# A grouped-query attention kernel: a third block of every job's exponentials on VectorE, converted inside its own job, with one step of the correction moved from GpSimd to VectorE in each second job

## The chip, the cores and the metric

The kernel runs on one core of one Trainium2 chip. The metric is the device time of one execution in microseconds (us); the number quoted for a kernel is the median of several runs. One execution is also recorded by the hardware profiler; its timeline is what the views below are taken from.

## What is computed

```python
batch, seq, n_heads, n_kv_heads, dim = 8, 512, 32, 8, 64
scale = 1.0 / np.sqrt(dim)
K_expanded = np.repeat(K, n_heads // n_kv_heads, axis=2)
V_expanded = np.repeat(V, n_heads // n_kv_heads, axis=2)
# each of Q, K_expanded, V_expanded then as (batch, heads, seq, dim)
scores = np.einsum('bhqd,bhkd->bhqk', Q, K_expanded) * scale
weights = np.exp(scores - np.max(scores, axis=-1, keepdims=True))
weights = weights / (np.sum(weights, axis=-1, keepdims=True) + 1e-10)
output = np.einsum('bhqk,bhkd->bhqd', weights, V_expanded)
return output.transpose(0, 2, 1, 3).astype(np.float32)
```

Softmax attention over 512 positions, 8 batches, 32 query heads; four query heads share one head of keys and values. Inputs and output are fp32.

## The kernel before, in words

**Jobs.** The work is cut into 64 jobs, j = 0 to 63, eight for each batch. A job is four query heads, as two pairs (`i` = 0, 1) of two heads (`m` = 0, 1). For each pair there are four key chunks of 128 (`kc`). One combination of i, kc and m is a block: scores of 128 keys by 512 queries, one PSUM bank. A job has 16 blocks. Scores stand with the keys on the partitions, so the exponentials can be used as the stationary operand of the second product without a transpose. No maximum is subtracted; sums that leave safe bounds would lead to a general path at the end, which does not run here.

**Two ways to an exponential.** Most blocks go through ScalarE (ACT): `act_tile` (L296) lets PE compute two blocks into an s tile (two PSUM banks, two buffers) and ACT write exp of 1024 columns to the fp16 tile `pt`. The first two or three blocks of a job's second pair go another way, through VectorE (DVE) and GpSimd (POOL). `exp_d` (L306) lets PE compute them into a d tile (two banks, one buffer), and VectorE converts the scores to an integer, `u`, whose bits are those of a fp16 number that is a rough exponential. `exp_d2` (L320) works out a correction: `f` takes the low ten bits of u (VectorE), `g` is a linear function of f (GpSimd, or VectorE where `odd` is true), `w` is the product of g and f (GpSimd). In the job that follows, `exp_d4` (L346) adds u and w into `pt` (VectorE). `WIDE` (L41) says in which jobs there are three blocks: those from 4 to 61 but for j % 5 = 2, 47 in all. `act_tiles` (L252) gives ACT the rest: seven tiles of two blocks in a job with two blocks on VectorE; with three, six such tiles and a half tile of one block.

**Second product.** `pv` (L365) multiplies `pt` of the job before (`last`) by the values, 32 products per pair. V has a column of ones, so the sums of the weights come out beside the output. All pairs share one pv tile (two banks, one buffer). `norm` (L402) reads it: a reciprocal of the sums (L417) and a multiplication into `o_sb` (L422), from where each second job a DMA on the SP queue stores 1 MB.

**Order.** The instructions of each engine run in the order in which the program writes them; there is no scheduler. The loop at L570 writes job j in this order: loads on the POOL queue that are due in this job (`LOADS`), transposes of keys on the SP queue (`dma_k`, `KEYS`), ACT tile 0, the d tile's first two blocks and their u, ACT tile 1, checks (`check_sums` looks at earlier sums, `check_v` at a part of V, both on VectorE), products of the last job's first pair around ACT tile 2, its norm, ACT tile 3. Then a second d tile, called `bank`: with three blocks, ACT's half tile goes to its second bank (`act_tile(j, 4, bank)`), and eight PE transposes of the Q of job j + 2 (`trans_q`, L207) go to its first. VectorE then has: add of the last job (L349), f (L325), the copy of the transposed Q out of the bank (L220), and g if it is VectorE's in this job (`rest`). PE goes on with products of the last job's second pair in parts (`cut`) around the tiles 5 and 6. If the next job has three blocks, the third of them is computed in this job already, into the second bank after ACT has read it, and VectorE converts it (L622). The norm of the second pair ends the job.

**Reuse.** Tiles wait for their readers: a new d tile for VectorE's and ACT's reads of the one before, a pv tile for the norm before. `apart` (L200) declares that two instructions are in different banks of one tile and need not wait for each other.

**Where g stands before.** `odd` is true in job 62 and in jobs with three blocks whose successor has two (6, 11, ... 56, 61).

Of the kernel before, what the change touches and what calls it, by code (L numbers as in the profile page):

```python
# [12 lines left out]
FP32 = mybir.dt.float32  # L13
BF16 = mybir.dt.bfloat16
# [23 lines left out]
LAST_SUMS = NLAST * 2 * 4  # L38


WIDE = lambda j: 4 <= j < 62 and j % 5 != 2  # L41


@with_exitstack
# [23 lines left out]
def fast_path(ctx, tc, Q, K, V, out, flag, ident):  # L68
# [78 lines left out]
    def d_tile():  # L147
        return d_pool.tile([128, 2, S], FP32, name="d_ps")
# [51 lines left out]
    def apart(this, other):  # L200
        if other is not None:
            tc.declare_no_dep(
                this.ins, other.ins, reason="the two are in different banks of one tile"
            )
        return this
# [40 lines left out]
    def taken(j):  # L246
        return 3 if WIDE(j) else 2

    def d_block(j):
        return SC * 2 - 2 if j == NJOB - 1 else 0  # L250

    def act_tiles(j):  # L252
# [7 lines left out]

    CHECKS = {
        (j, at): divmod(n, SC) for n, (j, at) in enumerate(
            [(j, 0) for j in (3, 4, 6, 7, 8, 11, 12, 16, 17, 21, 22, 23, 26, 27, 31, 32)]
            + [(j, 0) for j in (36, 37, 38, 41, 42, 46, 47, 48, 51, 52, 56, 57, 60, 61, 62)]
            + [(62, 1)]
        )
    }

    KEYS = dict(zip((4, 10, 16, 26, 36, 41, 50), range(1, B)))

    def in_jobs(load, first, jobs):
        for n, j in enumerate(jobs):
            LOADS.setdefault(j, []).append((load, first + n))

    LOADS = {1: [(load_q, 1, 0, 2 * HPG), (load_q, 1, 2 * HPG, 4 * HPG)]}
    in_jobs(load_k, 1, [3, 8, 12, 23, 32, 38, 48])
    in_jobs(load_q, 2, [3, 7, 8, 12, 17, 22, 23, 27, 32, 37, 38, 42, 47, 48])
    in_jobs(load_v, 1, [4, 13, 18, 28, 33, 43, 53])

    def scores(j, ps, i, kc, m):  # L280
        u, g = divmod(j, 2)
        b, gp = divmod(u, GP)
        keys = kt_first[:, gp, :, :] if u < 2 else kt[b][:, :, gp, :]
        return nc.tensor.matmul(  # L284
            ps,
            keys[64 * m:64 * m + 64, g if u == 0 else g ^ m, kc * 128:(kc + 1) * 128],
            qt[u][64 * m:64 * m + 64, g, i, :],
            start=True,
            stop=True,
        )  # L290
# [2 lines left out]
        pt = pt_pool.tile([128, NPAIR, SC, 2, S], FP16, name="pt")  # L293
        jobs.setdefault(j, {}).update(pt=pt, pv={})

    def act_tile(j, n, spare=None):  # L296
        group = act_tiles(j)[n]
        i, kc, lo = group[0]
        ps = s_pool.tile([128, 2, S], FP32, name="s_ps") if spare is None else spare
        for _, _, m in group:  # L300
            scores(j, ps[:, m, :], i, kc, m)
        return nc.scalar.activation(  # L302
            out=jobs[j]["pt"][:, i, kc, lo:, :], in_=ps[:, lo:, :], func=EXP, scale=scale
        )

    def exp_d(j, lo, hi, ps, other=None):  # L306
        st = jobs.setdefault(j, {})
        if "u" not in st:
            for name, dtype in (("u", I16), ("f", I16), ("g", BF16), ("w", BF16)):
                st[name] = dve_pool.tile([128, 3, S], dtype, name=name + "16")[:, 0:taken(j), :]  # L310
        for n in range(lo, hi):
            apart(scores(j, ps[:, n - lo, :], DPAIR, *divmod(d_block(j) + n, 2)), other)
        return lambda: nc.vector.tensor_scalar(  # L313
            out=st["u"][:, lo:hi, :], in0=ps[:, 0:hi - lo, :], scalar1=A_U, scalar2=B_U,
            op0=ALU.mult, op1=ALU.add,
        )

    def exp_d2(j, engine=None):  # L320
        st = jobs[j]
        by_bits = engine is None
        engine = engine or nc.gpsimd
        odd = j == NJOB - 2 or WIDE(j) and not WIDE(j + 1)
        nc.vector.tensor_single_scalar(  # L325
            out=st["f"], in_=st["u"], scalar=1023, op=ALU.bitwise_and
        )

        def factor():
            (nc.vector if odd else engine).tensor_scalar(  # L330
                out=st["g"], in0=st["f"], scalar1=-EXP_F1,
                scalar2=EXP_K * 2.0 ** (24 * by_bits), op0=ALU.add, op1=ALU.mult,
            )

        def product():
            engine.tensor_tensor(  # L336
                out=st["w"], in0=st["g"], in1=st["f"].bitcast(FP16) if by_bits else st["f"],
                op=ALU.mult,
            )

        if odd:
            return lambda: (factor(), product())
        factor()
        return product() if by_bits else product
# [210 lines left out]
    for filler in fillers:  # L555
        apart(copy, filler)
    two_keys(1)
    exp_d(0, 0, 2, d_tile())()
    act_tile(0, 3)
    act_tile(0, 4)  # L560
    exp_d2(0)
# [8 lines left out]
    for j in range(1, NJOB - 1):  # L570
        last = j - 1
        u, g = divmod(j, 2)
        b, gp = divmod(u, GP)
        open_job(j)
        if j == 1:
            nc.gpsimd.tensor_copy(out=gate, in_=jobs[0]["pt"][0:1, 0, SC - 1, 0, 0:1])
        for load, *of in LOADS.get(j, ()):
            load(*of)
        if j == 1:
            dma_k(0, 2)  # L580
        if j in KEYS:
            dma_k(KEYS[j])

        cut = (11, 19) if taken(j) < 3 else (4, 18) if taken(last) < 3 else (4, 16)
        act_tile(j, 0)
        if j == 1:
            piece(1, *first_k(1, 0, bank[:, 1, S // 2:]))
        exp_d(j, 0, 2, d_tile())()
        act_tile(j, 1)
        if j % 5 == 3:  # L590
            check_sums()
        if (j, 0) in CHECKS:
            check_v(*CHECKS[j, 0])
        pv(last, 0, 0, 16)
        act_tile(j, 2)
        pv(last, 0, 16, 32)
        norm(last, 0)
        act_tile(j, 3)

        reads = []  # L600
        bank = d_tile()
        beside = act_tile(j, 4, bank) if taken(j) > 2 else None

        ahead = (j + 1,) if j < 2 else (3, 4) if j == 2 else (j + 2,)
        for n, to in enumerate(ahead):
            if to < NJOB:
                reads.append(trans_q(to, bank[:, n, :], other=beside)[1])
        if j == 1:
            reads.append(first_k(1, 1, bank[:, 1, :])[1])
        exp_d4(last)  # L610
        rest = exp_d2(j)
        copies = [read() for read in reads]
        if rest:
            rest()
        if taken(j) == 2:
            act_tile(j, 4)
        pv(last, 1, 0, cut[0])
        act_tile(j, 5)
        if beside:
            pv(last, 1, *cut)  # L620
        if taken(j + 1) > 2:
            exp_d(j + 1, 2, taken(j + 1), bank[:, 1:2, :], copies[0])()  # L622
        if (j, 1) in CHECKS:
            check_v(*CHECKS[j, 1])
        if not beside:
            pv(last, 1, *cut)
        act_tile(j, 6)
        pv(last, 1, cut[1], 32)
        norm(last, 1)
        del jobs[last]  # L630
# [1 line left out]
    j, last = NJOB - 1, NJOB - 2  # L632
    open_job(j)
    act_tile(j, 0)
    exp_d(j, 0, 2, d_tile())()
    all_checks()
    act_tile(j, 1)
    pv(last, 0, 0, 16)
# [137 lines left out]
```

## Time and profile before

| | |
|---|---|
| median of 3 runs | 404.32 us (403.99 to 404.6) |
| the profiled execution, its time | 404.57 us |
| its span, first to last instruction | 402.8 us |
| PE: matmul busy, granted clock | 375.8 us (93%), 0.999 |
| PE weight loads busy | 228.0 us (57%) |
| ACT wide tiles (128x1024), count and mean | 400, 1122 ns |
| ACT half tiles (128x512), count and mean | 47, 724 ns |
| DMA over the span | 168 GB/s |

The profile gives for each engine the time in which at least one of its instructions ran. A record lasts until the engine's last write is acknowledged, and the next instruction starts before that, so records of one engine overlap: 400 ACT tiles of 1122 ns come to 379.0 us busy. For the pace of an engine the distance from start to start is read off the timeline. In a row of the timeline the columns are the start, the duration, the engine, the line, the operation, what is written and read, and the count; in brackets stands idle time of the engine ahead of it and what ended that. The chain of waits is followed back from the last instruction, at each step to what released it.

### The profile page before, as it was taken

What the parts mean: (1) busy time and instruction counts of PE and PEld (TensorE: products, weight loads), DVE (VectorE), ACT (ScalarE), POOL (GpSimd) and SP (SyncE); (2) the same over time, 40 slices, a digit from 0 to 9 for tenths busy, and PEclk for the clock granted to TensorE, in tenths of its full rate; (3) what the DMA queues carried; (4) which work ended last, traced back from release to release, by engine and by line L of the source; (5) the groups of instructions that cost most, each with busy time, mean ns of one, the idle gap of its engine ahead of it and who ended that gap; (6) DMA issues with size and microseconds to landing.
All of it is one profiled execution on the core that took longest, in us unless ns stands there. A gap on an engine that the chain in (4) does not pass through costs nothing.

```text
span 402.8 us, 12997 instructions
## 1 busy us (share of the span) xinstructions
PE 375.8 (93%) x5670; PEld 228.0 (57%) x5670; DVE 366.4 (91%) x635; ACT 393.9 (98%) x454; POOL 286.8 (71%) x169
## 2 busy tenths in 40 slices
PE   7999999999999999999999999999999999999985
PEld 3565555555555555555555555555555555556554
DVE  4788998999999999999999999999999999999996
ACT  5999999999999999999999999999999999999995
POOL 9848577597587687687687686677776767765752
PEclk9999999999999999999999999999999999999999
DMA  9979999899999259999259999679369959222206
GB/s 145 163 190 182 91 288 225 164 211 237 184 214 206 107 88 247 192 239 182 107 84 226 168 227 197 208 109 252 110 170 202 175 169 128 107 106 106 88 34 201
DMA packets 82893, 67.73 MB, mean 168 GB/s; under 512 B 52752, under 2 KB 57872, under 8 KB 82832
## 3 DMA queue, kind: packets, MB, share of 16 engines
q0 software_dynamic: 45072, 24.91, 48.3%
q1 hardware_dynamic: 36688, 41.49, 36.6%
q8 instruction: 45, 0.74, 0.7%
q10 hardware_dynamic: 1072, 0.46, 0.4%
q14 instruction: 16, 0.13, 0.1%
HBM read 50.33 MB, written 33.55 MB: 208 GB/s over the span
## 4 chain that ended last, share of the span: by engine, by line
ACT 29%; PE 25%; POOL 24%; DVE 20%; issue 2%; ACTq 0%; DVEq 0%
ACT pt L302 28%; POOL w L336 16%; PE pv L377 12%; PE s_ps L284 9%; POOL g L330 8%; DVE pt L349 8%; DVE o_sb L422 4%; DVE f L325 4%; DVE qt L220 2%; PE d_ps L215 2%; DVE g L330 1%; DVE inv L417 1%; PE d_ps L284 1%; PE s_ps L510 1%; PE d_ps L377 0%
## 5 line engine op out<-in xcount | busy, mean ns | idle before, releaser
L302 ACT ACTIVATE pt<-s_ps 128x1024 f16<-128x1024 f32 x400 | 379.0, 1122 | 0.3 <-PE s_ps L284 0.2
L336 POOL TENSOR_TENSOR w<-g,f 128x1536 bf16<-128x1536 bf16 (+1 forms) x63 | 179.6, 2851 | 37.6 <-DVE g L330 33.4
L377 PEld LDWEIGHTS <-pt 128*128 128x128 f16 x4096 | 142.1, 98 | 81.2 <-issue 41.6
L377 PE MATMUL pv<-v,pt 128*128 128x65 bf16 x4032 | 177.8, 195 | 3.7 <-DVE o_sb L422 2.2
L284 PE MATMUL s_ps<-qt,kt 64*128 64x512 bf16 x746 | 152.3, 384 | 12.0 <-ACT pt L302 10.0
L330 POOL TENSOR_SCALAR g<-f 128x1536 bf16<-128x1536 int16 (+1 forms) x50 | 67.1, 1341 | 69.1 <-DVE f L325 69.0
L313 DVE TENSOR_SCALAR u<-d_ps 128x1024 int16<-128x1024 f32 (+1 forms) x111 | 109.9, 990 | 0.3
L284 PEld LDWEIGHTS <-kt 64*128 64x128 bf16 x960 | 50.2, 93 | 55.3 <-issue 31.5
L422 DVE TENSOR_TENSOR o_sb<-pv,inv 128x512 f32<-128x512 f32 x112 | 77.5, 692 | 3.9
L284 PE MATMUL d_ps<-qt,kt 64*128 64x512 bf16 x214 | 58.4, 376 | 3.5 <-ACT pt L302 0.3
L349 DVE TENSOR_TENSOR pt<-u,w 128x1536 uint16<-128x1536 int16 (+1 forms) x64 | 56.4, 882 | 2.3 <-POOL w L336 0.2
L220 DVE COPY qt<-d_ps 128x1024 bf16<-128x1024 bf16 x62 | 42.3, 684 | 0.0
L215 PEld LDWEIGHTS <-q_nat 128*128 128x128 bf16 x508 | 28.5, 98 | 23.8 <-issue 23.8
L417 DVE RECIPROCAL inv<-pv 128x8 f32<-128x8 f32 x112 | 23.1, 207 | 17.4 <-PE pv L377 16.0
L215 PE MATMUL d_ps<-ident,q_nat 128*128 128x128 bf16 x496 | 38.3, 220 | 0.0
L302 ACT ACTIVATE pt<-d_ps 128x512 f16<-128x512 f32 x47 | 34.0, 724 | 0.0
L325 DVE TENSOR_SCALAR f<-u 128x1536 int16<-128x1536 int16 (+1 forms) x64 | 33.3, 521 | 0.0
L238 DVE TENSOR_REDUCE okv<-v 128x1 f32<-128x512 bf16 x32 | 21.6, 676 | 0.0
L142 POOL DMA_DIRECT2D q_nat<-in_Q_dram x19 | 15.2, 801 | 0.1
L284 PE MATMUL s_ps<-qt,kt_first 64*128 64x512 bf16 x56 | 11.1, 396 | 1.9 <-ACT pt L302 1.5
L127 POOL DMA_DIRECT2D v<-in_V_dram x7 | 12.3, 1753 | 0.0
L422 DVE TENSOR_TENSOR o_sb<-pv,inv_last 128x512 f32<-128x512 f32 x14 | 9.7, 692 | 0.5
(61 smaller groups left out, 62.7 us busy)
## 6 DMA issues: line engine op xcount, KB each, us to landing
out_dram<-o_sb SPq DMA_DIRECT2D x31, 1024.0 KB, 6.1
q_nat<-in_Q_dram POOLq DMA_DIRECT2D x14, 1024.0 KB, 12.4
k_nat<-in_K_dram POOLq DMA_DIRECT2D x7, 512.0 KB, 7.5
v<-in_V_dram POOLq DMA_DIRECT2D x7, 512.0 KB, 13.6
kt<-kt SPq DMA_DIRECT2D x14, 256.0 KB, 4.0
q_nat<-in_Q_dram POOLq DMA_DIRECT2D x3, 512.0 KB, 7.5
out_dram<-o_sb SPq DMA_DIRECT2D x3, 256.0 KB, 2.4
kt<-k_nat SPq DMA_TRANSPOSE x32, 5.9
```

Of the source, the lines that this page charges most:

```text
L215: nc.tensor.transpose(ps[:, i, sc, :], qn[u // 2][:, sc, h:h + 2, :], ident),
L220: return done, lambda: apart(nc.vector.tensor_copy(out=qt[u][:, g, lo:hi, :], in_=ps[:, lo:hi, :, :].rearrange("p i sc c -> p i (sc c)")), ...
L284: return nc.tensor.matmul(ps, keys[64 * m:64 * m + 64, g if u == 0 else g ^ m, kc * 128:(kc + 1) * 128], qt[u][64 * m:64 * m + 64, g, i, : ...
L302: return nc.scalar.activation(out=jobs[j]["pt"][:, i, kc, lo:, :], in_=ps[:, lo:, :], func=EXP, scale=scale)
L313: return lambda: nc.vector.tensor_scalar(out=st["u"][:, lo:hi, :], in0=ps[:, 0:hi - lo, :], scalar1=A_U, scalar2=B_U, op0=ALU.mult, op1=AL ...
L325: nc.vector.tensor_single_scalar(out=st["f"], in_=st["u"], scalar=1023, op=ALU.bitwise_and)
L330: (nc.vector if odd else engine).tensor_scalar(out=st["g"], in0=st["f"], scalar1=-EXP_F1, scalar2=EXP_K * 2.0 ** (24 * by_bits), op0=ALU.a ...
L336: engine.tensor_tensor(out=st["w"], in0=st["g"], in1=st["f"].bitcast(FP16) if by_bits else st["f"], op=ALU.mult,)
L349: nc.vector.tensor_tensor(out=st["pt"][:, DPAIR, :, :, :].rearrange("p kc m q -> p (kc m) q")[:, d_block(j):d_block(j) + n, :].bitcast(U16 ...
L377: nc.tensor.matmul(st["pv"][i][:, m, qc, :], st["pt"][:, i, kc, m, qc * 128:(qc + 1) * 128], vt[b % 2][:, kc, 2 * gp + g, :], start=(n < 2 ...
L417: nc.vector.reciprocal(out=inv, in_=sums[:, :, :, D:D + 1])
L422: nc.vector.tensor_tensor(out=osb[u][:, :, h:h + 2, :].rearrange("p qc m d -> p m qc d"), in0=sums[:, :, :, 0:D], in1=inv[:, :, :, None].t ...
```

## The change

`WIDE` loses its exception: all 58 jobs from 4 to 61 have three blocks on VectorE. A new `ALONE` puts g on VectorE in every even job from 4 on. The third block is no longer computed in the job before: `odd_tile` takes the second d tile of the job itself, computes the third block into its first bank and ACT's single block into its second; ACT reads the one and VectorE converts the other. ACT tiles 5 and 6 and twelve products of the last job's second pair follow on PE, and only then the transposes of Q, into the first bank. On VectorE the order is now u of the third block, add, f, g (if even), copy of Q. The remaining 20 products of the second pair come in one piece at the job's end. The lists of checks, of key transposes and of loads are written anew: the checks of V in odd jobs, the checks of sums where j % 8 = 2, from job 6 on in even jobs alone and one per job, but for job 8 with two (before, in jobs of both kinds, and two in six of them). Nothing else differs.

```diff
@@ -38,7 +38,10 @@
 LAST_SUMS = NLAST * 2 * 4
 
 
-WIDE = lambda j: 4 <= j < 62 and j % 5 != 2
+WIDE = lambda j: 4 <= j < 62
+
+
+ALONE = lambda j: j >= 4 and j % 2 == 0
 
 
 @with_exitstack
@@ -260,22 +263,20 @@
 
     CHECKS = {
         (j, at): divmod(n, SC) for n, (j, at) in enumerate(
-            [(j, 0) for j in (3, 4, 6, 7, 8, 11, 12, 16, 17, 21, 22, 23, 26, 27, 31, 32)]
-            + [(j, 0) for j in (36, 37, 38, 41, 42, 46, 47, 48, 51, 52, 56, 57, 60, 61, 62)]
-            + [(62, 1)]
+            [(j, 0) for j in range(3, 62, 2)] + [(62, 0), (62, 1)]
         )
     }
 
-    KEYS = dict(zip((4, 10, 16, 26, 36, 41, 50), range(1, B)))
+    KEYS = {8 * b + 2 if b else 4: b + 1 for b in range(B - 1)}
 
     def in_jobs(load, first, jobs):
         for n, j in enumerate(jobs):
             LOADS.setdefault(j, []).append((load, first + n))
 
     LOADS = {1: [(load_q, 1, 0, 2 * HPG), (load_q, 1, 2 * HPG, 4 * HPG)]}
-    in_jobs(load_k, 1, [3, 8, 12, 23, 32, 38, 48])
-    in_jobs(load_q, 2, [3, 7, 8, 12, 17, 22, 23, 27, 32, 37, 38, 42, 47, 48])
-    in_jobs(load_v, 1, [4, 13, 18, 28, 33, 43, 53])
+    in_jobs(load_k, 1, [3, 8] + [8 * b + 2 for b in range(1, B - 2)])
+    in_jobs(load_q, 2, [3, 6] + [8 * b + n for b in range(1, B - 1) for n in (0, 6)])
+    in_jobs(load_v, 1, [4] + [8 * b + 4 for b in range(1, B - 1)])
 
     def scores(j, ps, i, kc, m):
         u, g = divmod(j, 2)
@@ -293,35 +294,46 @@
         pt = pt_pool.tile([128, NPAIR, SC, 2, S], FP16, name="pt")
         jobs.setdefault(j, {}).update(pt=pt, pv={})
 
-    def act_tile(j, n, spare=None):
+    def act_tile(j, n):
         group = act_tiles(j)[n]
         i, kc, lo = group[0]
-        ps = s_pool.tile([128, 2, S], FP32, name="s_ps") if spare is None else spare
+        ps = s_tile()
         for _, _, m in group:
             scores(j, ps[:, m, :], i, kc, m)
         return nc.scalar.activation(
             out=jobs[j]["pt"][:, i, kc, lo:, :], in_=ps[:, lo:, :], func=EXP, scale=scale
         )
 
-    def exp_d(j, lo, hi, ps, other=None):
-        st = jobs.setdefault(j, {})
-        if "u" not in st:
-            for name, dtype in (("u", I16), ("f", I16), ("g", BF16), ("w", BF16)):
-                st[name] = dve_pool.tile([128, 3, S], dtype, name=name + "16")[:, 0:taken(j), :]
-        for n in range(lo, hi):
-            apart(scores(j, ps[:, n - lo, :], DPAIR, *divmod(d_block(j) + n, 2)), other)
-        return lambda: nc.vector.tensor_scalar(
-            out=st["u"][:, lo:hi, :], in0=ps[:, 0:hi - lo, :], scalar1=A_U, scalar2=B_U,
-            op0=ALU.mult, op1=ALU.add,
-        )
-
-
+
+    def odd_tile(j, ps):
+        (i, kc, m), = act_tiles(j)[4]
+        scores(j, ps[:, 0, :], i, kc, 0)
+        scores(j, ps[:, m, :], i, kc, m)
+        st = jobs[j]
+        left = nc.scalar.activation(
+            out=st["pt"][:, i, kc, m:, :], in_=ps[:, m:, :], func=EXP, scale=scale
+        )
+        apart(to_bits(st["u"][:, 2:3, :], ps[:, 0:1, :]), left)
+        return left
+
+    def to_bits(out, in_):
+        return nc.vector.tensor_scalar(
+            out=out, in0=in_, scalar1=A_U, scalar2=B_U, op0=ALU.mult, op1=ALU.add
+        )
+
+    def exp_d(j, ps):
+        st = jobs[j]
+        for name, dtype in (("u", I16), ("f", I16), ("g", BF16), ("w", BF16)):
+            st[name] = dve_pool.tile([128, 3, S], dtype, name=name + "16")[:, 0:taken(j), :]
+        for n in range(2):
+            scores(j, ps[:, n, :], DPAIR, *divmod(d_block(j) + n, 2))
+        to_bits(st["u"][:, 0:2, :], ps)
 
     def exp_d2(j, engine=None):
         st = jobs[j]
         by_bits = engine is None
         engine = engine or nc.gpsimd
-        odd = j == NJOB - 2 or WIDE(j) and not WIDE(j + 1)
+        odd = ALONE(j)
         nc.vector.tensor_single_scalar(
             out=st["f"], in_=st["u"], scalar=1023, op=ALU.bitwise_and
         )
@@ -555,7 +567,7 @@
     for filler in fillers:
         apart(copy, filler)
     two_keys(1)
-    exp_d(0, 0, 2, d_tile())()
+    exp_d(0, d_tile())
     act_tile(0, 3)
     act_tile(0, 4)
     exp_d2(0)
@@ -581,13 +593,13 @@
         if j in KEYS:
             dma_k(KEYS[j])
 
-        cut = (11, 19) if taken(j) < 3 else (4, 18) if taken(last) < 3 else (4, 16)
+        cut = (12, 12) if taken(j) > 2 else (11, 19)
         act_tile(j, 0)
         if j == 1:
             piece(1, *first_k(1, 0, bank[:, 1, S // 2:]))
-        exp_d(j, 0, 2, d_tile())()
+        exp_d(j, d_tile())
         act_tile(j, 1)
-        if j % 5 == 3:
+        if j % 8 == 2:
             check_sums()
         if (j, 0) in CHECKS:
             check_v(*CHECKS[j, 0])
@@ -599,7 +611,12 @@
 
         reads = []
         bank = d_tile()
-        beside = act_tile(j, 4, bank) if taken(j) > 2 else None
+        beside = None
+        if taken(j) > 2:
+            beside = odd_tile(j, bank)
+            act_tile(j, 5)
+            pv(last, 1, 0, cut[0])
+            act_tile(j, 6)
 
         ahead = (j + 1,) if j < 2 else (3, 4) if j == 2 else (j + 2,)
         for n, to in enumerate(ahead):
@@ -609,22 +626,18 @@
             reads.append(first_k(1, 1, bank[:, 1, :])[1])
         exp_d4(last)
         rest = exp_d2(j)
-        copies = [read() for read in reads]
         if rest:
             rest()
-        if taken(j) == 2:
-            act_tile(j, 4)
-        pv(last, 1, 0, cut[0])
-        act_tile(j, 5)
-        if beside:
-            pv(last, 1, *cut)
-        if taken(j + 1) > 2:
-            exp_d(j + 1, 2, taken(j + 1), bank[:, 1:2, :], copies[0])()
+        for read in reads:
+            read()
         if (j, 1) in CHECKS:
             check_v(*CHECKS[j, 1])
         if not beside:
+            act_tile(j, 4)
+            pv(last, 1, 0, cut[0])
+            act_tile(j, 5)
             pv(last, 1, *cut)
-        act_tile(j, 6)
+            act_tile(j, 6)
         pv(last, 1, cut[1], 32)
         norm(last, 1)
         del jobs[last]
@@ -632,7 +645,7 @@
     j, last = NJOB - 1, NJOB - 2
     open_job(j)
     act_tile(j, 0)
-    exp_d(j, 0, 2, d_tile())()
+    exp_d(j, d_tile())
     all_checks()
     act_tile(j, 1)
     pv(last, 0, 0, 16)
```

## Prediction

> **What bounds the kernel now.** I read the page's busy times first, then the chain of waits by engine, then the busy times of the stretch that holds jobs 4 to 61, and last the timelines of single jobs. From the page, section 1 and the shares of the chain:
>
> ```profile
> span 402.8 us, 12997 instructions
> ...
> PE 375.8 (93%) x5670; PEld 228.0 (57%) x5670; DVE 366.4 (91%) x635; ACT 393.9 (98%) x454; POOL 286.8 (71%) x169
> ...
> ACT 29%; PE 25%; POOL 24%; DVE 20%; issue 2%; ACTq 0%; DVEq 0%
> ```
>
> ACT looks full, yet only 29% of the chain that ended last runs through it. The stretch from the first conversion of job 4 to that of job 62 shows why the busy column misleads (its columns: stretch, length, then busy and count of PE, PEld, DVE, ACT, POOL; below it are the two DVE rows that bound the stretch, and three rows of ACT):
>
> ```profile
> 32.25:385.45 353.20, 335.23 (x5105) 203.29 (x5104) 331.45 (x567) 353.07 (x408) 255.30 (x131) 1.00 0.86 170
> ...
> 32.25 1.21 DVE L313 TENSOR_SCALAR u<-d_ps 128x1024 int16<-128x1024 f32 x1
> ...
> 385.45 1.22 DVE L313 TENSOR_SCALAR u<-d_ps 128x1024 int16<-128x1024 f32 x1
> ...
> 206.67 5.66 ACT L302 ACTIVATE pt<-s_ps 128x1024 f16<-128x1024 f32 x6
> 212.09 0.72 ACT L302 ACTIVATE pt<-d_ps 128x512 f16<-128x512 f32 x1
> 212.57 5.75 ACT L302 ACTIVATE pt<-s_ps 128x1024 f16<-128x1024 f32 x6
> ```
>
> 58 jobs take 353.20 us, 6.09 each. ACT's records overlap their successors, so I count from start to start: six wide tiles in 212.09 - 206.67 = 5.42, so 0.903 each, and a half tile in 212.57 - 212.09 = 0.48. A job with three blocks on VectorE needs 6 x 0.903 + 0.48 = 5.90 us of ACT, one with two blocks 7 x 0.903 = 6.32. With 47 and 11 of them ACT needs 5.98 per job. It is close to the bound, but 0.11 short of 6.09.
>
> The other 0.11 comes from VectorE's own order. One job of it, complete, with the start of the next:
>
> ```profile
> 214.88 1.21 DVE L313 TENSOR_SCALAR u<-d_ps 128x1024 int16<-128x1024 f32 x1
> 216.66 0.21 DVE L417 RECIPROCAL inv<-pv 128x8 f32<-128x8 f32 x1 [0.57 <-PE pv L377]
> 216.91 0.69 DVE L422 TENSOR_TENSOR o_sb<-pv,inv 128x512 f32<-128x512 f32 x1
> 217.51 0.95 DVE L349 TENSOR_TENSOR pt<-u,w 128x1536 uint16<-128x1536 int16 x1
> 218.38 0.55 DVE L325 TENSOR_SCALAR f<-u 128x1536 int16<-128x1536 int16 x1
> 218.85 0.69 DVE L220 COPY qt<-d_ps 128x1024 bf16<-128x1024 bf16 x1
> 219.45 0.68 DVE L313 TENSOR_SCALAR u<-d_ps 128x512 int16<-128x512 f32 x1
> 220.09 0.21 DVE L417 RECIPROCAL inv<-pv 128x8 f32<-128x8 f32 x1
> 220.34 0.69 DVE L422 TENSOR_TENSOR o_sb<-pv,inv 128x512 f32<-128x512 f32 x1
> 220.94 1.22 DVE L313 TENSOR_SCALAR u<-d_ps 128x1024 int16<-128x1024 f32 x1
> ```
>
> From start to start the steps are: u of two blocks and the wait behind it 1.78, reciprocal 0.25, norm (o_sb) 0.60, add 0.87, f 0.47, copy of Q 0.60, u of the third block 0.64, reciprocal 0.25, norm 0.60. Their sum is 6.06. The reader is to see that there is one idle spot, 0.57, and that it is no reserve. What it waits for is on PE:
>
> ```profile
> 221.08 0.66 PE L377 MATMUL pv<-v,pt 128*128 128x65 bf16 x16
> 221.67 0.39 PE L284 MATMUL s_ps<-qt,kt 64*128 64x512 bf16 x2
> 221.99 0.66 PE L377 MATMUL pv<-v,pt 128*128 128x65 bf16 x16
> ```
>
> There is one pv tile. The second norm of a job frees it at 220.34 + 0.69 = 221.03, PE starts the next pair's products at 221.08, and they end at 222.65. So VectorE and PE hand the tile to and fro, and every instruction that VectorE has between the first reciprocal and the second norm lengthens the job by its whole duration, while 1.78 us after the second norm are fixed. A check of V fits into those:
>
> ```profile
> 227.09 1.22 DVE L313 TENSOR_SCALAR u<-d_ps 128x1024 int16<-128x1024 f32 x1
> 228.22 0.68 DVE L238 TENSOR_REDUCE okv<-v 128x1 f32<-128x512 bf16 x1
> 228.86 0.21 DVE L417 RECIPROCAL inv<-pv 128x8 f32<-128x8 f32 x1
> ```
>
> With the check the step is 1.77, as long as without.
>
> A second loop runs through GpSimd: f, g and w of one job, then the add in the next.
>
> ```profile
> 219.02 1.47 POOL L330 TENSOR_SCALAR g<-f 128x1536 bf16<-128x1536 int16 x1 [1.63 <-DVE f L325]
> 220.58 3.10 POOL L336 TENSOR_TENSOR w<-g,f 128x1536 bf16<-128x1536 bf16 x1
> ...
> 223.71 0.96 DVE L349 TENSOR_TENSOR pt<-u,w 128x1536 uint16<-128x1536 int16 x1
> 224.58 0.55 DVE L325 TENSOR_SCALAR f<-u 128x1536 int16<-128x1536 int16 x1
> ```
>
> From f (218.38) to the next add (223.71) are 5.33 us; with the add it is 6.20 per job wherever GpSimd does g and w in a row. So three loops lie at 5.98, 6.06 and 6.20, and 6.09 is their mixture.
>
> **The change part by part.**
>
> Third block on VectorE in 11 more jobs (7, 12, ... 57). ACT needs 5.90 in all 58 jobs, so 11 x 0.42 = 4.6 us less. On VectorE each of the 11 gains a u of the third block, and f and add work on 1536 columns. The wide job above has these already, so its 6.06 is the length that I give to a job without g.
>
> g on VectorE in each even job. Before, g stood there in jobs whose successor has two blocks, and thus in jobs that have no u of a third block at that place:
>
> ```profile
> 231.25 0.69 DVE L220 COPY qt<-d_ps 128x1024 bf16<-128x1024 bf16 x1
> 231.85 0.55 DVE L330 TENSOR_SCALAR g<-f 128x1536 bf16<-128x1536 int16 x1
> 232.32 0.20 DVE L417 RECIPROCAL inv<-pv 128x8 f32<-128x8 f32 x1
> ```
>
> It costs 232.32 - 231.85 = 0.47 and was paid by the 0.64 that was missing there. After the change an even job has both. An odd job stays at 6.06, an even one takes 6.06 + 0.47 = 6.53. The 0.47 lies between first reciprocal and second norm; the 0.57 of idle time lies outside of that and can't take it. Both together are 12.59.
>
> The wait for GpSimd. From an even job, w alone is on GpSimd and comes early. From an odd job it takes the 5.33 of above. VectorE's road from f (odd) to the next add is f 0.47, copy 0.60, reciprocal and norm 0.85, 1.78, 0.85, u of the third block 0.64: 5.19. So the add waits 0.14 there. The whole round is 5.33 to the add, then add 0.87, f 0.47, g 0.47, copy 0.60, 0.85, 1.78, 0.85, u 0.64, add 0.87, which are 7.40. The sum is **12.73 us for two jobs**. What was good for the loop through GpSimd (6.20 on end no more) is lost to the loop through the pv tile.
>
> Third block in its own job, in one bank beside ACT's half tile. PE's two scores for it come one after the other behind s tile 3; VectorE is at its norm then. No row shows VectorE and ACT on the two banks of one tile at once. I take the 0.64 of the same u on a bank of its own; as bounds, 0.60 (the best overlap of a record of this size with the next, as the copy's 219.45 - 218.85) and 0.68 (none), so 58 x 0.04 = 2.3 either way. The Q transposes now follow this u and two tiles of ACT, and the copy follows add and f: VectorE reaches it 0.87 + 0.47 = 1.34 after the add starts (1.81 with g). PE needs half of that for the transposes, which may start when u ends:
>
> ```profile
> 217.09 0.62 PE L215 MATMUL d_ps<-ident,q_nat 128*128 128x128 bf16 x8
> ```
>
> I cost it at nothing. If that cover goes, PE is late (a rival below).
>
> Of the copy's new place: the scores for the next u wait for it. It ends 0.69 after its start, and the norm ends 0.60 + 0.25 + 0.69 = 1.54 after it. PE has two pairs of scores to issue in between, 0.32 each (221.99 - 221.67), so it is ready some 0.2 before the pv tile is free. No cost, with 0.2 to spare.
>
> Checks of sums, now in jobs with j % 8 = 2: two more instructions behind u.
>
> ```profile
> 209.86 0.76 DVE L388 SCALAR_TENSOR_TENSOR ok<-inv,ok 128x128 f32<-128x128 f32 x2
> 210.65 0.21 DVE L417 RECIPROCAL inv<-pv 128x8 f32<-128x8 f32 x1
> ```
>
> The start to start step from u at 208.73 is 1.92, 0.14 over 1.78; these jobs are even, so the 0.14 falls into the wait for GpSimd. No cost. Checks of V move to odd jobs, where the 1.78 hides them.
>
> Loads. They stand in even jobs from 6 on, one per job (job 8 has K and Q, together less than a V), behind w of the job before. GpSimd is then free until g of VectorE ends, 0.87 + 0.47 + 0.47 = 1.81 after the add starts. The longest, V, takes 1.76:
>
> ```profile
> 205.72 0.77 POOL L142 DMA_DIRECT2D q_nat<-in_Q_dram  x1
> ...
> 206.24 0.50 DVE L325 TENSOR_SCALAR f<-u 128x1024 int16<-128x1024 int16 x1
> ...
> 210.09 1.76 POOL L127 DMA_DIRECT2D v<-in_V_dram  x1
> ...
> v<-in_V_dram POOLq DMA_DIRECT2D x7, 512.0 KB, 13.6
> ```
>
> It fits, and w of an even job has room: VectorE's way from g's end to the next add is 0.60 + 0.85 + 1.78 + 0.85 + 0.64 = 4.72, and w takes 3.10. The shortest lead of a load is three jobs, some 18 us, against 13.6 from issue to landing for V, the last row. The key transposes on SP start six jobs ahead of their use, as the first of them do now. No cost; I allow 0 to 1 us for loads that collide with stores.
>
> A rule of the Trainium skill speaks against this place for the loads: "SBUF — State Buffer", section "Who interferes with whom", has VectorE in a two-port mode and GpSimd shut each other out for a whole instruction. By it the V issue, which starts first, would hold f until it ends, 1.76 - 0.87 = 0.89 late, in seven jobs: 6.2 us. The rows above speak against it: f started while the Q issue still had 0.25 to run, and was done 0.25 after that issue; held, it would have started no sooner than 206.49.
>
> Ends. Job 4 has an add of two blocks and no wait for GpSimd: -0.4. Job 3 loses a u, but has two blocks and stays by ACT's 6.32: 0. Job 62 waits for w of job 61, whose g is on GpSimd now: 5.33 - (0.47 + 0.60 + 0.85 + 1.78 + 0.85 = 4.55), +0.8, of which I take 0.6, since its check of V can wait beside it.
>
> Sum: 29 x 12.73 = 369.2 for jobs 4 to 61, 16.0 more than 353.2, and 0.2 for the ends, so +16.2. The profiled execution took 404.57 (402.8 and 1.77 around it), which gives 420.8; the median of the runs is 0.25 lower. **420.5 us**, slower by 4%.
>
> **The rivals.**
>
> PE late. The 0.2 to spare after the copy is only four times the 0.05 that PE took from the end of a norm to its start (221.03 to 221.08). If PE misses it by 0.15 in each job, 58 x 0.15 = 8.7 more: 429. For it: 20 pv products in a row now stand behind transposes. Against: the jobs are longer than ACT's 5.90 by 0.16 and 0.77, so its tiles come free early for PE.
>
> The lock of the issue: if a V issue holds f, 6.2 more, 427. Against it the f above.
>
> A part of g hidden. If g shortens the wait for GpSimd more than I think, and half of the 0.47 finds another wait, 29 x 0.24 = 7 less: 413.
>
> Not slower: VectorE's wait for pv closes. If PE gets the pv tile 0.57 sooner in even jobs, g is paid: 29 x 0.57 = 16.5 less, 404. The point is the one pv tile: it would have to be free before the second norm has read it, which the order excludes. VectorE's work alone sets a floor here: 331.45 in the stretch, 11 times 0.64 and at most a third of 0.87 and of 0.47, 12.0, and 17 more g at 0.47, 8.0, make 351.4 of 353.2.
>
> ACT decides. If ACT is the bound and the rest follows, 58 jobs at 5.90 are 342.2, 11 less: 393.6. For it the 98%. By the Trainium skill, "Perfetto Trace Analysis", section "Identifying the Most-Contended Engine", the engine with the highest occupancy is the one to relieve, which is what this change does. Against it, VectorE's floor of 351.4 is above 342.2, and 29% of the chain.
>
> **How the numbers follow.** The forecast has 0.70, with its own range of 416 (no wait for GpSimd, 29 x 0.14 = 4 less) to 424 (0.04 for u and a little more in each job). PE late 0.12, the lock 0.04, half of g hidden 0.05, wait closed 0.05, ACT 0.04. I let the range run from 413 to 427, which leaves out ACT, the closed wait and most of late PE. A measurement of this kernel tells 0.2%, some 0.8 us, from no change. Faster: ACT and a part of the closed wait, 0.06. Same: 0.03. Slower: 0.91.
>
> **What would show it.** Right: starts of u of two blocks alternate between some 6.06 (odd) and 6.67 (even); ACT shows gaps of some 0.4 per job; the reciprocal still waits about half a microsecond for pv in even jobs; the add in even jobs waits 0.1 to 0.2 for w. Wrong: jobs under 6.2 on average, or a wait of u or pv for scores (PE late), or f that starts late beside a V issue.

## The result and the profile after

| | before | changed |
|---|---|---|
| median | 404.37 us (403.99 to 404.6, 4 runs) | 444.03 us (443.28 to 446.27, 4 runs) |
| ratio | | 1.0991, 95% interval 1.0948 to 1.1034 |
| the profiled execution | 404.57 us, span 402.8 | 446.27 us, span 444.5 |

Slower by 39.7 us, where 16.2 were forecast. From the page of the changed kernel, the lines that answer to those of before:

```profile
span 444.5 us, 13036 instructions
...
PE 375.0 (84%) x5670; PEld 231.0 (52%) x5670; DVE 402.2 (90%) x663; ACT 397.1 (89%) x454; POOL 276.4 (62%) x152
...
PEclk9999989899999999899998989989999899998999
...
DVE 54%; POOL 21%; PE 9%; DMA 6%; issue 5%; ACT 3%; SPq 1%; POOLq 0%; ACTq 0%; DVEq 0%
...
L400 DVE SCALAR_TENSOR_TENSOR ok<-inv,ok 128x128 f32<-128x128 f32 x14 | 19.3, 1378 | 0.2
```

ACT has left the chain (3% after 29%), VectorE holds 54% of it, and TensorE's clock dips. One group stands out: the checks of sums take 1378 ns each, 19.3 us in all, where the same 14 instructions took 0.28 to 0.44 before. Nothing about them was changed but their job.

An even job without check or V load, on VectorE:

```profile
114.07 1.21 DVE L320 TENSOR_SCALAR u<-d_ps 128x1024 int16<-128x1024 f32 x1
115.83 0.21 DVE L429 RECIPROCAL inv<-pv 128x8 f32<-128x8 f32 x1 [0.55 <-PE pv L389]
...
116.68 0.68 DVE L320 TENSOR_SCALAR u<-d_ps 128x512 int16<-128x512 f32 x1
117.55 0.96 DVE L361 TENSOR_TENSOR pt<-u,w 128x1536 uint16<-128x1536 int16 x1 [0.18 <-POOL w L348]
118.42 0.55 DVE L337 TENSOR_SCALAR f<-u 128x1536 int16<-128x1536 int16 x1
119.01 0.56 DVE L342 TENSOR_SCALAR g<-f 128x1536 bf16<-128x1536 int16 x1
119.48 0.68 DVE L223 COPY qt<-d_ps 128x1024 bf16<-128x1024 bf16 x1
...
120.93 1.21 DVE L320 TENSOR_SCALAR u<-d_ps 128x1024 int16<-128x1024 f32 x1
```

It takes 120.93 - 114.07 = 6.86; the odd job ahead of it began at 108.10 and took 5.97. The pair is 12.83 to 12.84, where 12.73 were forecast: the idle 0.55 for pv, the wait for w and g's 0.47 are all there. This part of the forecast stands. What it had at nothing is in single jobs. A job with a check, j = 10, VectorE and then GpSimd:

```profile
72.83 1.22 DVE L320 TENSOR_SCALAR u<-d_ps 128x1024 int16<-128x1024 f32 x1
73.96 2.79 DVE L400 SCALAR_TENSOR_TENSOR ok<-inv,ok 128x128 f32<-128x128 f32 x2
76.67 0.20 DVE L429 RECIPROCAL inv<-pv 128x8 f32<-128x8 f32 x1
...
81.83 1.22 DVE L320 TENSOR_SCALAR u<-d_ps 128x1024 int16<-128x1024 f32 x1
```

```profile
73.19 3.09 POOL L348 TENSOR_TENSOR w<-g,f 128x1536 bf16<-128x1536 bf16 x1
76.22 0.60 POOL L117 DMA_DIRECT2D k_nat<-in_K_dram  x1
```

The checks start at 73.96, inside w, and end at 76.75, just after w ends at 76.28. The first of the two takes 2.46 of the 2.79 and ends some 0.15 after w, in this job and in the six others. The job takes 9.00. A job with a V load, j = 12, GpSimd and then VectorE:

```profile
91.20 1.75 POOL L130 DMA_DIRECT2D v<-in_V_dram  x1
```

```profile
91.29 0.96 DVE L361 TENSOR_TENSOR pt<-u,w 128x1536 uint16<-128x1536 int16 x1 [0.19 <-POOL w L348]
92.17 1.15 DVE L337 TENSOR_SCALAR f<-u 128x1536 int16<-128x1536 int16 x1
93.34 0.56 DVE L342 TENSOR_SCALAR g<-f 128x1536 bf16<-128x1536 int16 x1
```

f takes 1.15 instead of 0.55 and ends 0.37 after the V issue (92.95). And in job 8 the scores wait for keys (PE):

```profile
58.68 0.39 PE L285 MATMUL s_ps<-qt,kt 64*128 64x512 bf16 x1 [2.04 <-DMA kt<-kt]
```

The stretch of jobs 4 to 61 is 394.49 us long after the change and 353.20 before. The forecast had 369.2. Job lengths, from start to start of the u of two blocks, add up to the difference as follows; the first row compares with the forecast, the others with plain jobs of the changed kernel (5.97 odd, 6.87 even):

| jobs | length, us | more than expected, us |
|---|---|---|
| all pairs | 12.84, not 12.73 | 29 x 0.11 = 3.2 |
| 10, 18, ... 58, with checks | 8.65 to 9.13, not 6.87 | 62.1 - 48.1 = 14.0 |
| 12, 20, ... 52, with a V load | 7.45 to 7.47, not 6.87 | 44.75 - 41.22 = 3.5 |
| 7 and 8, around the late keys | 7.86 and 7.50, not 5.97 and 6.87 | 2.5 |
| 37 | 6.96, not 5.97 | 1.0 |

That is 24.2 of the 25.3 us missing; five odd jobs behind a check, 0.03 to 0.41 longer each, have 1.1. Jobs 4 and 56 (6.56 and 7.18) cancel.

### The profile page after: what moved, and what is told of

Read it like the earlier page. It is cut to its first block, busy times and chain, and to the rows that moved or that the text cites. A ratio compares the mean times of both kernels' runs of the same rounds, so it can differ in the third digit from the quotient of the medians.

```text
span 444.5 us, 13036 instructions
## 1 busy us (share of the span) xinstructions
PE 375.0 (84%) x5670; PEld 231.0 (52%) x5670; DVE 402.2 (90%) x663; ACT 397.1 (89%) x454; POOL 276.4 (62%) x152
## 4 chain that ended last, share of the span: by engine, by line
DVE 54%; POOL 21%; PE 9%; DMA 6%; issue 5%; ACT 3%; SPq 1%; POOLq 0%; ACTq 0%; DVEq 0%
POOL w L348 14%; DVE u L320 12%; DVE pt L361 10%; DVE o_sb L434 8%; POOL g L342 7%; DVE f L337 6%; DVE ok L400 4%; PE pv L389 4%; DVE qt L223 4%; DVE okv L241 3%; ACT pt L303 3%; DVE g L342 3%; DMA kt<-k_nat 2%; PE s_ps L285 2%; DVE inv L429 2%
## 5 line engine op out<-in xcount | busy, mean ns | idle before, releaser
L303 ACT ACTIVATE pt<-s_ps 128x1024 f16<-128x1024 f32 x389 | 373.3, 1050 | 38.8 <-PE s_ps L285 32.9
L348 POOL TENSOR_TENSOR w<-g,f 128x1536 bf16<-128x1536 bf16 (+1 forms) x63 | 189.8, 3013 | 63.0 <-DVE g L342 60.3
L389 PEld LDWEIGHTS <-pt 128*128 128x128 f16 x4096 | 149.1, 100 | 100.5 <-DVE o_sb L434 73.5
L285 PE MATMUL s_ps<-qt,kt 64*128 64x512 bf16 x724 | 146.0, 395 | 5.8 <-ACT pt L303 2.6
L320 DVE TENSOR_SCALAR u<-d_ps 128x1024 int16<-128x1024 f32 x122 | 117.3, 961 | 1.9 <-PE d_ps L285 1.8
L342 POOL TENSOR_SCALAR g<-f 128x1536 bf16<-128x1536 int16 (+1 forms) x33 | 46.7, 1416 | 96.0 <-DVE f L337 95.9
L285 PE MATMUL d_ps<-qt,kt 64*128 64x512 bf16 x236 | 47.3, 391 | 19.9 <-DVE qt L223 17.7
L337 DVE TENSOR_SCALAR f<-u 128x1536 int16<-128x1536 int16 (+1 forms) x64 | 38.2, 597 | 0.0
L400 DVE SCALAR_TENSOR_TENSOR ok<-inv,ok 128x128 f32<-128x128 f32 x14 | 19.3, 1378 | 0.2
L342 DVE TENSOR_SCALAR g<-f 128x1536 bf16<-128x1536 int16 (+1 forms) x31 | 17.1, 552 | 1.1
```

The lines of the kernel that those rows point to most:

```text
L285: return nc.tensor.matmul(ps, keys[64 * m:64 * m + 64, g if u == 0 else g ^ m, kc * 128:(kc + 1) * 128], qt[u][64 * m:64 * m + 64, g, i, : ...
L303: return nc.scalar.activation(out=jobs[j]["pt"][:, i, kc, lo:, :], in_=ps[:, lo:, :], func=EXP, scale=scale)
L320: return nc.vector.tensor_scalar(out=out, in0=in_, scalar1=A_U, scalar2=B_U, op0=ALU.mult, op1=ALU.add)
L337: nc.vector.tensor_single_scalar(out=st["f"], in_=st["u"], scalar=1023, op=ALU.bitwise_and)
L342: (nc.vector if odd else engine).tensor_scalar(out=st["g"], in0=st["f"], scalar1=-EXP_F1, scalar2=EXP_K * 2.0 ** (24 * by_bits), op0=ALU.a ...
L348: engine.tensor_tensor(out=st["w"], in0=st["g"], in1=st["f"].bitcast(FP16) if by_bits else st["f"], op=ALU.mult,)
```

## The experiments

**Theory H** (hold): a VectorE instruction of certain kinds, beside a GpSimd instruction that began before it, is held until that one ends, and its record gets longer. Checks (two inputs in SBUF) are held by w, f by the issue of a load. **Rivals**: the checks are slow by themselves (S), the half clock costs the time (C), and further ones named in the expectations.

| run | median, us | ratio to before, 95% interval |
|---|---|---|
| e1_sums_moved | 434.2 | 1.0725, 1.07 to 1.075 |
| e2_loads_odd | 438.96 | 1.0854, 1.0836 to 1.0872 |
| e3_both_moved | 429.89 | 1.0629, 1.0593 to 1.0665 |
| e4_before_sums | 412.13 | 1.019, 1.0173 to 1.0207 |
| e5_copy_between | 425.81 | 1.0517, 1.05 to 1.0535 |
| e6_g_on_pool | 419.34 | 1.0362, 1.0345 to 1.038 |
| e7_check_v_late | 436.55 | 1.0794, 1.0776 to 1.0812 |
| e8_before_wide | 421.78 | 1.0429, 1.0411 to 1.0446 |
| e9_before_thirds | 408.3 | 1.0095, 1.0079 to 1.0112 |
| e10_before_halves | 411.85 | 1.0187, 1.017 to 1.0204 |

### Checks of sums behind the add

```diff
-        if j % 8 == 2:
-            check_sums()
...
         exp_d4(last)
+        if j % 8 == 2:
+            check_sums()
         rest = exp_d2(j)
```

> The changed kernel with one edit: the checks of sums go from behind the first u of their job to behind the add, in the same jobs (j % 8 = 2). Theory H (hold): there they stand beside w on GpSimd, and VectorE's two-input instruction is held until w ends; behind the add GpSimd has no w running. Each pair then takes 0.76 as before the change and not 2.79, the seven jobs go from some 9.0 to 7.6 us, and the time from 444 to about 434. Rival S (the checks are slow by themselves now, through what their job does): the pair stays at 2.8 and the time at 443 to 445, or grows, since the 0.6 us of idle time that hid a part of them is gone. Rival C (TensorE's half clock is what costs): the time falls only as far as the share of half clock falls.

434.2 us, 9.8 less than the changed kernel. VectorE in job 10:

```profile
76.89 0.96 DVE L361 TENSOR_TENSOR pt<-u,w 128x1536 uint16<-128x1536 int16 x1 [0.19 <-POOL w L348]
77.77 0.61 DVE L400 SCALAR_TENSOR_TENSOR ok<-inv,ok 128x128 f32<-128x128 f32 x2
```

The same two instructions on the same data take 0.61, not 2.79, and job 10 takes 7.41, not 9.00. S falls.

### Loads in odd jobs

```diff
-    in_jobs(load_k, 1, [3, 8] + [8 * b + 2 for b in range(1, B - 2)])
-    in_jobs(load_q, 2, [3, 6] + [8 * b + n for b in range(1, B - 1) for n in (0, 6)])
-    in_jobs(load_v, 1, [4] + [8 * b + 4 for b in range(1, B - 1)])
+    in_jobs(load_k, 1, [3, 9] + [8 * b + 3 for b in range(1, B - 2)])
+    in_jobs(load_q, 2, [3, 7] + [8 * b + n for b in range(1, B - 1) for n in (1, 7)])
+    in_jobs(load_v, 1, [4] + [8 * b + 5 for b in range(1, B - 1)])
```

> The changed kernel with one edit: every load from job 6 on is issued one job later, in odd jobs, so behind the w of an even job, when GpSimd idles and VectorE runs neither f nor g. Theory H: f beside a V issue falls from 1.15 to 0.55, V's jobs from 7.46 to 6.87, seven times 0.59 = 4.1. Besides, Q's load of job 6 no longer runs beside the copies of keys that job 8 needs: the 2 us of PE's wait for kt go, and job 7 falls from 7.9 to 6.0. Together 437 to 438. Rival N (the row of before read as it was in the prediction: an issue does not hold f): f stays, 441 to 442 from the keys alone. Rival K (the keys are late through the SP queue, not the load): job 7 stays at 7.9, 440.

438.96 us, 5.1 less, a microsecond above the expectation. The V load of job 13 on GpSimd, and the next f:

```profile
94.05 1.75 POOL L130 DMA_DIRECT2D v<-in_V_dram  x1
```

```profile
96.35 0.55 DVE L337 TENSOR_SCALAR f<-u 128x1536 int16<-128x1536 int16 x1
```

The issue ends at 95.80, before f starts, and no f is longer than 0.56 in the run. Job 12 takes 6.88, job 7 takes 5.97, job 8 6.87: V's hold and the wait for keys are both gone. For the keys this shows that a load one job earlier made them late (Q's issue at 47.99, the key copies' at 49.53); by which queue or DMA engine was not separated.

### Both

The edits of the two runs together.

> The changed kernel with the edits of both runs before: checks of sums behind the add, loads in odd jobs. Theory H: nothing on VectorE that reads or writes SBUF by two ways stands beside GpSimd any more; what is left is the round of two jobs, 12.84 us in the changed kernel (12.73 by the prediction), 29 times, and seven checks at 0.76: 425 to 428, granted clock back at 0.99 or more. Rival C (the clock falls because PE idles in every even job): the clock stays below 0.98 and the time above 432.

429.89 us, 14.1 less than the changed kernel; the single savings of 9.8 and 5.1 add up to 14.9, as near as the run's spread (428.19 to 431.18) can tell. The profiled clock is 0.994. The pairs stay at 12.84 and check jobs at 7.40. C falls as the main cause: the time follows the held instructions and the clock recovers with them. The 2 us above the expectation come from its sum: 29 x 12.84 = 372.4, the 51.4 outside of jobs 4 to 61 and 0.53 more for each job with checks are 427.5 already. The rest is in single odd jobs, above all job 43 (7.11, with a clock dip, below), and at the ends.

### The same hold made in the kernel before

```diff
-        if j % 5 == 3:
+        if j % 5 == 4:
             check_sums()
```

> The kernel before with one edit: the checks of sums from jobs with j % 5 = 3 to j % 5 = 4, that is one job later. In the job before the old place w has two blocks and ends early; before the new one w has three blocks and runs until the add. Theory H: the pair takes 1.8 to 2.0 instead of 0.76, seven jobs get longer by 1.0 to 1.3, 411 to 413. Rival S: the pair stays at 0.76 and the time at 404 to 405.

412.13 us. VectorE, and w on GpSimd, in job 19:

```profile
125.61 1.87 DVE L388 SCALAR_TENSOR_TENSOR ok<-inv,ok 128x128 f32<-128x128 f32 x2
127.39 0.20 DVE L417 RECIPROCAL inv<-pv 128x8 f32<-128x8 f32 x1
```

```profile
123.91 3.09 POOL L336 TENSOR_TENSOR w<-g,f 128x1536 bf16<-128x1536 bf16 x1
```

One number changed and 7.8 us lost. w ends at 127.00, the checks at 127.48, and the profiled clock is 1.0, so the hold costs this time without any dip. The old place followed a job with two blocks, whose w ends early.

### The copy of Q between f and g

```diff
+        for read in reads:
+            read()
         if rest:
             rest()
-        for read in reads:
-            read()
```

On top of both moves.

> The kernel of the third run (both moved) with one edit: in even jobs the copy of Q goes back between f and g, as in the kernel before. In the changed kernel f to g takes 0.59 from start to start, where f to the copy takes 0.47. Theory D (g waits for the end of f, since it reads it at once): the 0.12 goes, even jobs fall from 6.87 to 6.75, 29 times, 3.5 us, so 426 to 427. w starts 0.6 later, which has room. Rival: f is longer there for another reason (loads, GpSimd), and the even jobs stay at 6.87, 429 to 431.

425.81 us, 4.1 less. VectorE in an even job:

```profile
113.97 0.55 DVE L337 TENSOR_SCALAR f<-u 128x1536 int16<-128x1536 int16 x1
114.44 0.68 DVE L223 COPY qt<-d_ps 128x1024 bf16<-128x1024 bf16 x1
115.04 0.55 DVE L342 TENSOR_SCALAR g<-f 128x1536 bf16<-128x1536 int16 x1
115.51 0.20 DVE L429 RECIPROCAL inv<-pv 128x8 f32<-128x8 f32 x1
```

f and g now cost 0.47 each and even jobs take 6.74. g right behind f had to wait for f's end.

### g on GpSimd

```diff
-ALONE = lambda j: j >= 4 and j % 2 == 0
+ALONE = lambda j: j == 62
```

On top of both moves.

> The kernel of the third run with one edit: g on GpSimd in all jobs but 62. Theory H with its loops: VectorE's order is 5.97 in each job, the round through GpSimd (f, g, w, add) takes 6.20, so all jobs take 6.20 and a check's job 0.6 to 0.8 more, since the checks stand in that round: 58 x 6.20 + 5 = 365 for jobs 4 to 61 against 377, 416 to 419 in all. So g on VectorE costs 0.2 per job net, and the wide jobs alone still lose against 6.09. Rival B (g on VectorE relieves GpSimd, and the jobs are longer for other reasons): 430 or more.

419.34 us; all plain jobs take 6.19 to 6.22. So g on VectorE costs 0.22 per job net (12.84 / 2 - 6.20), 12.8 us in 58 jobs. The run is 10.6 us faster than the third and not 12.8, for in six jobs (6.78 or 6.79) the V issue stands beside f again, since w ends late. That the round through GpSimd is what leaves 6.20 fits its length in the prediction; no run varies it alone. Job 21:

```profile
144.23 1.14 DVE L337 TENSOR_SCALAR f<-u 128x1536 int16<-128x1536 int16 x1
```

```profile
143.27 1.75 POOL L130 DMA_DIRECT2D v<-in_V_dram  x1
```

### The check of V outside of the wait

```diff
-            [(j, 0) for j in range(3, 62, 2)] + [(62, 0), (62, 1)]
+            [(j, int(j > 4)) for j in range(3, 62, 2)] + [(62, 0), (62, 1)]
```

On top of both moves.

> The kernel of the third run with one edit: the checks of V in odd jobs go from behind the first u to behind the copy of Q, ahead of the second reciprocal. Theory of the pv tile: behind u they lie in VectorE's wait for PE and cost nothing; between first reciprocal and second norm the same instruction costs its whole 0.64, less the 0.18 that even jobs now wait for w: 0.4 to 0.45 per pair of jobs, 12 to 13 us, 441 to 444. Rival (VectorE is simply near full, and a place is as good as another): 429 to 431.

436.55 us, 6.7 more than with the same instructions in the old place, half of what I expected. An odd job's end and its successor's start:

```profile
215.84 0.68 DVE L223 COPY qt<-d_ps 128x1024 bf16<-128x1024 bf16 x1
216.44 0.67 DVE L241 TENSOR_REDUCE okv<-v 128x1 f32<-128x512 bf16 x1
217.03 0.20 DVE L429 RECIPROCAL inv<-pv 128x8 f32<-128x8 f32 x1
```

Odd jobs grow from 5.97 to 6.57, by the check's whole 0.59. Even jobs shrink from 6.87 to 6.58, for they no longer wait for w; that wait was worth 0.29, more than the 0.18 of idle time that the row shows, because the idle time counts from the end of a record that the next instruction would have overlapped. That makes 0.31 per pair, 9.0 in all; the third run's single long jobs (27, 43, 56) are not seen here. The direction fits the pv tile's loop; the size missed was the wait for w.

### Three blocks in all jobs, and nothing else

```diff
-WIDE = lambda j: 4 <= j < 62 and j % 5 != 2
+WIDE = lambda j: 4 <= j < 62
```

In the kernel before.

> The kernel before with one edit: three blocks in all jobs from 4 to 61, the rest of its order and its lists as they were (g is on VectorE in jobs 61 and 62 alone). Theory H: all jobs run in the round through GpSimd, 6.20, 58 times 359.6; the seven checks of sums now stand beside a w of three blocks and are held, 1.0 each: 366 to 367 against 353, 417 to 419. Rival A (ACT is the bound, 98% busy): 58 x 5.90, 393 to 395.

421.78 us, 3 above the expectation. Plain jobs take 6.20 and those with checks 7.39. Where K and Q are issued in one job, six times, f is held to 0.77, which I had not counted; the held checks cost 1.2 each and not 1.0.

### Fewer jobs with three blocks

```diff
-WIDE = lambda j: 4 <= j < 62 and j % 5 != 2
+WIDE = lambda j: 4 <= j < 62 and j % 3 != 2
...
-    in_jobs(load_v, 1, [4, 13, 18, 28, 33, 43, 53])
+    in_jobs(load_v, 1, [4, 12, 18, 27, 33, 42, 51])
...
-        if j % 5 == 3:
+        if j % 3 == 0:
             check_sums()
```

> The kernel before with its pattern of jobs changed: two blocks on VectorE in every third job (j % 3 = 2) and not in every fifth. Checks of sums and V's loads go to jobs that follow one with two blocks, as before (j % 3 = 0), so that neither stands beside a w of three blocks. Theory H with its loops: in three jobs one takes 5.98 (two blocks), one 6.13 and one 6.07 (g on VectorE, no u of a third block), 6.06 on average against 6.09; ACT needs 6.04. 58 x 0.03 = 1.7 less: 402 to 403.5. Rival A (ACT is the bound already): ACT needs 6.04 and not 5.98 on average, 58 x 0.06 more, 407 to 408.

> As the run before, with two blocks in every odd job from 5 on, checks of sums in even jobs and V's loads in even jobs. Theory H: VectorE's loops would give 5.98 and 6.07, 6.02 on average, but ACT needs (5.90 + 6.32) / 2 = 6.11: here ACT is the bound, 58 x 0.02 more than before, 405 to 407. Rival (VectorE's order alone decides): 400 to 401.

The second has `j % 2 != 1`, checks in even jobs and V at 4, 14, 18, 28, 34, 44, 54. Both missed: 408.3 and 411.85 us. ACT in the first:

```profile
202.02 12.21 ACT L302 ACTIVATE pt<-s_ps 128x1024 f16<-128x1024 f32 x13
213.81 0.91 ACT L302 ACTIVATE pt<-d_ps 128x512 f16<-128x512 f32 x1
```

13 tiles in 213.81 - 202.02 = 11.79, 0.907 each, which is ACT at full pace. The stretch of jobs 4 to 61 is 355.94 and 359.82 long, 6.14 and 6.20 per job. ACT needs 6.04 and 6.11. Before it was 6.09 with 5.98. So in all three the job is ACT's need and some 0.1: rival A of the first of these two runs was right, and the second came out above its expectation, which had set ACT's bare need of 6.11 against a measured 6.09. The kernel before is thus best read as bound by ACT with a small loss at the handovers, VectorE's 6.06 right beside it, and not as the mixture of VectorE's loops that the prediction had. The prediction's own row agrees: ACT's records cover 353.07 of 353.20 us. The 0.1 is spread over ACT's tiles (before, the 359 wide ones of the stretch follow each other at 0.920 on average, 0.904 at best); what delays them was not separated. No version tried beats it.

## Why the prediction was right or wrong

**Right: the direction, and the round of two jobs.** The one pv tile makes VectorE and PE take turns; the even job's idle 0.55 could not take g; the odd job's g on GpSimd makes the next add wait. 12.84 against 12.73. The two sizes that were off: g cost 0.59 for its place behind f (forecast 0.47, shown by the fifth run), and the wait for w 0.27 to 0.29 (forecast 0.14; in the even job above, u to add is 0.87 instead of 0.60). The u of the third block, 0.60 and not 0.64, made up for some.

**Wrong: "Checks of sums ... the 0.14 falls into the wait for GpSimd. No cost."** This step failed most. It took the check's duration from a job in which it stands beside the end of a short w, and moved it beside a long one. That w in the kernel before, on GpSimd:

```profile
208.02 2.12 POOL L336 TENSOR_TENSOR w<-g,f 128x1024 bf16<-128x1024 bf16 x1
```

It ends at 210.14. Of the two checks that begin at 209.86, the first ends at 210.30, so even the 0.76 held a short hold; away from w the pair takes 0.61 (first run). Beside the long w the checks cost 2.0 us in each of seven jobs, clock dips included; moving them gave 9.8 us back, and moving them beside a long w in the kernel before cost 7.8.

**Wrong: the lock, given 0.04.** The prediction cited the rule of the Trainium skill ("SBUF — State Buffer", section "Who interferes with whom"), priced only V's issue by it, and set it aside on a row: f started at 206.24, before the Q issue ended at 206.49. But a record's start is no sign against a hold. In the changed kernel f starts at 92.17 as well, inside the V issue, and is held all the same: what moves is its end, 0.37 after the issue's. Read by its end, the row of before agrees: 206.74, 0.25 after the issue's end, with a third less to do. Its 0.50 is itself long: 14 of the 17 f of this size take 0.42, and this one and the other beside a Q issue take 0.50 and 0.48. The rule's other half, that an instruction with two inputs in SBUF is held by a GpSimd instruction that reads it, is what the checks show, and that half I did not apply at all. By the prediction's working of the rule V would have cost 0.89 per job; the runs show 0.59.

**Wrong in size: loads that collide, "0 to 1 us".** 2.5 us in jobs 7 and 8, gone when the loads move one job on. The lead was misread too: the prediction has the key transposes begin six jobs ahead, but those for job 8 begin in job 4.

**Wrong in what bounds the kernel before**, without weight for the result: ACT, not VectorE's order, by what the last two runs indicate. The rule of "Perfetto Trace Analysis" in the Trainium skill, on the engine with the highest occupancy, agrees with that: ACT's busy share is 98%, the highest. What the rule does not tell is what comes next. ACT does get 11 wide tiles less and 11 half tiles more (389 and 58 in the profile, 400 and 47 before), 4.6 us by the prediction's estimate, but the loops at 6.20 (g on GpSimd) or 6.42 (g on VectorE in turn) lie above.

**The rivals.** PE late: not seen as a rule, u waits for scores once in the changed kernel, 1.80 us at 59.32, where the keys are late. Half of g hidden, the wait closed, ACT decides: all three would have made the change cheaper than the forecast, free or faster, and the pair came out at 12.84, longer than the 12.73.

What is left of the change when holds, loads and the copy are mended, 425.81 against 404.37, is 21.4 us. The round of two jobs has 15.1 of it (29 x 12.70 = 368.3 against 353.2), near the 16.0 of the forecast; 3.7 are the jobs with checks (7.27 instead of 6.74), 1.1 is one odd job with a clock dip, and the rest lies in other single jobs and at the ends.

## What to carry to other kernels

When an instruction is moved, look at what the neighbour engine does at the new place: a duration measured beside an idle or ending GpSimd does not hold beside a running one. To find a hold, compare the ends of two records and the longest duration of a group with its median, not their starts. And an idle spot in a loop of two engines is only worth something to instructions that may run there: here that was the check of V, with one input, but neither g nor a check of sums.

## What the runs showed of the hardware

A held VectorE instruction shows no idle time and starts when it would have; its record grows (0.28 to 2.46 for a check, 0.55 to 1.15 for f). The end gives the hold away. In all 28 jobs of the changed kernel and of the second, fourth and eighth runs, the first check of the pair ends 0.14 to 0.15 us after w, wherever inside w it began. f of 1536 columns ends some 0.36 after a V issue. The add, with two inputs in SBUF, is not held by an issue: it takes 0.96 inside the V issue (91.29 above) and 0.95 or 0.96 elsewhere. One f at the start of the program, which began 0.06 to 0.20 us after an issue did, was not held (0.43, in the first, fourth, sixth and eighth runs); why is open.

TensorE's granted clock halves for a stretch when PE has been less busy, without an idle time of that length. The half clock comes in stretches of 3.41 us that begin at whole multiples of 3.41 us from each other (in the changed kernel nine, at 60.13, 77.20, 131.81 and so on). In the third run there is one, in job 43: the windows of most of job 42, of the 3.41 us right before the dip, and of the first half of job 43 (the number behind the length is PE's busy time, the last three columns are the granted clock, the DMA share and GB/s), and then PE's own rows:

```profile
279.00:285.67 6.67, 5.06 (x75) 2.86 (x72) 5.79 (x13) 5.80 (x8) 4.00 (x2) 1.00 1.17 169
282.46:285.87 3.41, 1.79 (x28) 0.84 (x25) 3.31 (x9) 2.54 (x4) 1.48 (x1) 1.00 1.19 191
285.67:289.10 3.43, 3.29 (x38) 2.18 (x40) 2.45 (x5) 2.12 (x3) 2.34 (x2) 0.53 0.51 107
```

```profile
284.96 0.39 PE L285 MATMUL d_ps<-qt,kt 64*128 64x512 bf16 x2 [1.20 <-DVE qt L223]
...
285.81 1.04 PE L389 MATMUL pv<-v,pt 128*128 128x65 bf16 x16 [0.24 <-DVE o_sb L434]
...
292.92 0.67 PE L389 MATMUL pv<-v,pt 128*128 128x65 bf16 x16 [0.16 <-DVE o_sb L434]
```

For 3.4 us 16 products take 1.04 instead of 0.67, the pv handover is late, and this odd job takes 7.11 instead of 5.97. The longest gap of PE ahead of it was 1.20, and PE was busy 1.79 of the 3.41 us right before. Counted over jobs 4 to 61 of all runs, every dip follows 3.41 us with 1.23 to 1.91 us of busy time; after more than 1.91 there is none, and after 1.83 and 1.87 in the second run there is none either, so a limit near 1.9 is indicated and not settled. In the changed kernel seven of the nine dips stand in the jobs with held checks, one behind the late keys and one behind the V issue of job 36: a hold keeps PE waiting, and the slow clock comes on top.

The Trainium skill ("TensorE: Matmul & The Clock Gate", section "What's actually happening") has the clock fall after an idle window of some 3.4 us. The length of the dip agrees; the condition does not, for PE was busy 1.23 to 1.91 of the 3.41 us ahead of these dips.
